# Two mixture-of-experts routers: what is gathered, in which precision, and in what portions

## The chip, the core and the metric

The kernel runs on one core of one Trainium2 chip. The metric is device time in microseconds (us) of one launch. The kernel before took 1326.77 us, the median of three runs (1324.72, 1326.77, 1327.38). Each traced run is one execution recorded by the hardware profiler.

## The reference

Two stacked transformer blocks work on 256 tokens of width 1024. Each block ends in a hierarchical mixture of experts (MoE). What matters here is that MoE; block 1 has 16 experts with hidden width 256, block 2 has 32 experts with hidden width 512:

```
h   = rms_norm(x) * gain (+ shift in block 2)
g   = softmax(h @ w_group + b_group)          # 4 groups, the best one is taken, p_g its probability
e   = h @ w_router + b_router                 # experts of that group only; the two best, softmax of the two
out = sum over the two experts:  p_g * p_e * (silu(h @ w_gate[e]) * (h @ w_up[e])) @ w_down[e]
x   = x + (gate of the block) * out
```

`rms_norm(x)` is x times r, where r = 1/sqrt(mean(x^2) + eps), one number per token. It is the "root" of this case. Block 2 takes the adaptive gains, shifts and gates of its norms from a conditioning vector, by twelve products with a 1024 x 6144 matrix that are here called ada jobs.

## The kernel before, in words

**Order of the work.** Block 1 mixes (0 to 137 us), adds `w_out` (to 148), routes (to 173) and runs its MoE (to 308). Block 2 mixes until 837 us, routes until 859 and runs its MoE until 1312; a final norm ends the program. Every engine runs its instructions in the order in which a scheduler put them; `with after(i):` pins an instruction behind another. SP (SyncE) issues the weight transfers one after the other in a fixed order (`Stream.ahead`, `Stream.take`). Each is a 1 MB tile that goes to one of 19 buffers of 8 KB a partition, tag `g8`; in the same 19 lie x, the transposed h (`hTm`), `xnl` and `XT`. A transfer waits until its buffer's last reader is done. A second pool, `st4`, has 4 smaller buffers.

**A router** (`Router`, then the head of `moe`). x is transposed on TensorE (`ptm`) and evicted as `hTm`; `plg` are the logits; DVE works out r (`rsqrt`) and applies it to the logits (`lg`). A chain of some 20 small DVE operations finds the two experts of a token (`f1m`, `f1o`, `f2m`, `f2o`) and ends in the one-hot rows `Mr` (L1013). TensorE counts places with `Mr`: `ppos`, five fp32 matmuls against a triangle and a matrix of ones. An fp32 matmul stands as two rows of TensorE in the trace, an fp32r matmul or a transpose as one; the text calls such a row a pass. From `ppos` comes `pe`, the place of a token in its expert's 64 slots or -1.

**Dispatch** (`places`, `dispatch`). `Dd` is a one-hot matrix (token by slot) from comparing `pe` with a row of numbers. `pgx` multiplies x*r by `Dd`, so each expert's tokens stand transposed in `XT`. x*r is carried as two fp32r halves, `xnh` (ACT, L956, after r) and the rest `xnl` (POOL, L1029 and L1030, for one half of the tokens, DVE, L1034, for the other). Four experts (a quad, two pairs) are dispatched at a time: 4 PSUM tiles x 2 x 4 matmuls of 256 columns, so 32 passes. `pgt` transposes `Dd` back into `Gt`, and `pws` gathers the weights of the slots (`ws`).

**Pairs.** For each pair of experts PE does gate (`pgg`, `pgu` in block 1), the turn of the previous pair's activations (`pactT`), its `pdn`, then up (`pgu`) and the combination of the previous pair (`py`, L1203). Behind each second pair stands the next dispatch. Two matrices of 256 x 4 KB of `XT` alternate.

**Ada jobs** (`ada_job`, L600). `pada` leaves four partial sums on four groups of partitions; ACT copies them (`adap`), four transposes `pac` (four more, `paq`, with columns taken in steps of four, in four of the jobs) turn them, and DVE reduces and adds. Six jobs run in block 1's mixing, three around the first router, three in block 2's mixing.

Of the kernel before, what the change touches and what calls it, by code (L numbers as in the profile page):

```python
# [10 lines left out]
F32 = mybir.dt.float32  # L11
# [10 lines left out]
D = 1024  # L22
KD = 8
# [45 lines left out]
C1_N = C_MB + 1024  # L69
# [3 lines left out]
def _consts():  # L73
# [11 lines left out]
    c[:, C_IOTA:C_IOTA + 64] = np.arange(64)  # L85
# [37 lines left out]
def _body(es, tc, I, cst_d, msk_d, out_d, tap, stop):  # L123
# [43 lines left out]
    ones = cst[:, C_ONE:C_ONE + 128]  # L167
# [281 lines left out]
    class Router:  # L449


        def __init__(self, x, E, gw, gb, ew, eb, gcol, bcol):
            self.x, self.E, self.gcol = x, E, gcol
            wr = self.wr = S("wr", [KD, 36], bufs=1)
# [5 lines left out]
            self.hTm = None  # L460
# [8 lines left out]
        def half(self, n):  # L469
# [131 lines left out]
    def ada_job(jobs, b, step=False):  # L601
# [4 lines left out]
        def run(t0, t1):  # L606
# [10 lines left out]
            q = mm_ps("pac", (4, 4, 32))  # L617
# [16 lines left out]

    fgq = by_four("fgq", I["ffn_norm_g"][0])
# [23 lines left out]
    for b in range(ADA1):  # L659
        ada_job(J1, b)  # L660
    for n in range(2):
        J1.row32(I["w_out"][0], 512 * n, lambda: mix[0],
               lambda j, p, n=n: V.tensor_tensor(x1[j][:, 512 * n:512 * n + 512], p,
                                                 xr[j][:, 512 * n:512 * n + 512], op=ALU.add))
# [8 lines left out]
    A.dma_start(cst[:, C_J:C_N], cst_d[:, C_J:C_N])  # L673
    J1.ahead(2)
# [41 lines left out]
    lam = S("lam", [1], bufs=1)  # L716

# [181 lines left out]
    def both(*gens):  # L899
        gens = list(gens)  # L900
        while gens:
            for g in list(gens):
# [22 lines left out]
    x1 += xt_  # L925
    st1.ahead(PRE1)
    drain(J1.run(2))
    rt = Router(x1, 16, I["router_g_w"][0], I["router_g_b"][0], I["router_e_w"][0], I["router_e_b"][0],
                colA[:, oFG:oFG + 8], None)
    for n in range(2):  # L930
        rt.half(n)
    for n in range(2):
        rt.logits(n)
# [5 lines left out]
    def moe(x, E, router, gcol, bcol, st, FE, n_static, mid=None, before_if=None, gain=None, idle=None):  # L939
# [5 lines left out]
        xh = [sp.tile([128, 2, 512], F32R, tag="st4", name="xnh", bufs=NST).rearrange("p a b -> p (a b)")  # L945
              for _ in range(2)]
        xl = R2("xnl", F32R)
        def q4(v, n=2):

            return v.rearrange("p (h k c) -> p h c k", h=n, k=4)  # L950

        def c4(v, n=2):
            return v.rearrange("p (h c k) -> p h c k", h=n, k=4)

        for i in (1, 0):
            A.activation(q4(xh[i]), c4(x[i]), AF.Copy, scale=r[:, i:i + 1])  # L956
# [37 lines left out]
        V.tensor_reduce(gpr, gx, op=ALU.add, axis=AX.X)  # L994
        V.reciprocal(gpr, gpr)
# [9 lines left out]
        w1 = S("w1", [2])  # L1005
        V.tensor_scalar(w1, e2, 1.0, None, op0=ALU.add)
        V.reciprocal(w1, w1)
        V.tensor_tensor(w1, w1, gpr, op=ALU.mult)
        V.tensor_tensor(e2, e2, w1, op=ALU.mult)
        pe = S("pe", [2, 40], bufs=1)  # L1010
        we = S("we", [2, 40], bufs=1)
        M = S("Mr", [2, E], bufs=1)
        last_m = V.tensor_tensor(M, oh1, oh2, op=ALU.add)  # L1013
        V.tensor_tensor(oh1, oh1, b3(w1, E), op=ALU.mult)
        V.tensor_tensor(oh2, oh2, b3(e2, E), op=ALU.mult)
        V.tensor_tensor(we[:, :, 0:E], oh1, oh2, op=ALU.add)

        ppx = mm_ps
        pp = ppx("ppos", (3, E))
        lt = cst[:, C_LT:C_LT + 128]  # L1020
        mm(pp[:, 0, :], lt, M[:, 0, :], True, True)
        mm(pp[:, 1, :], lt, M[:, 1, :], True, False)
        mm(pp[:, 1, :], ones, M[:, 0, :], False, True)
        mm(pp[:, 2, :], ones, M[:, 0, :], True, False)
        pos = mm(pp[:, 2, :], ones, M[:, 1, :], False, True)
        for n in range(2):
            cs = slice(512 * n, 512 * n + 512)
            t = W("xn", [512])
            G.tensor_scalar(t, x[1][:, cs], r[:, 1:2], None, op0=ALU.mult)  # L1029
            G.tensor_tensor(q4(xl[1][:, cs], 1), c4(t, 1), q4(xh[1][:, cs].bitcast(F32), 1), op=ALU.subtract)  # L1030
        with after(last_m):
            for n in range(2):
                cs = slice(512 * n, 512 * n + 512)
                V.scalar_tensor_tensor(q4(xl[0][:, cs], 1), c4(x[0][:, cs], 1), r[:, 0:1],  # L1034
                                       q4(xh[0][:, cs].bitcast(F32), 1), op0=ALU.mult, op1=ALU.subtract)
# [4 lines left out]
        V.scalar_tensor_tensor(pe[:, :, 0:E], pp[:, 0:2, :], 1.0, M, op0=ALU.add, op1=ALU.mult)  # L1040
        V.tensor_scalar(pe[:, :, 0:E], pe[:, :, 0:E], 1.0, None, op0=ALU.subtract)
# [4 lines left out]
        def spill():  # L1046
# [28 lines left out]
            V.tensor_scalar(s2_, s2_, -float(CAP), 1.0 - CAP, op0=ALU.mult, op1=ALU.add)  # L1075
# [6 lines left out]
            V.tensor_scalar(pe[:, :, E:NE], pe[:, :, E:NE], 1.0, None, op0=ALU.subtract)  # L1082
# [4 lines left out]
        def places(e0, n):  # L1087
            d = W("Dd", [2, n, 64], F32R)
            it = cst[:, C_IOTA:C_IOTA + 64].unsqueeze(1).to_broadcast([128, n, 64])
            for i in range(2):  # L1090
                V.tensor_tensor(d[:, i], it, pe[:, i, e0:e0 + n].unsqueeze(2).to_broadcast([128, n, 64]), op=ALU.is_equal)
            return d

        def dispatch(e0, n, xt=None, d=None, late=None):
# [935 lines left out]
```

## Time and profile before

| | us |
|---|---|
| median of 3 runs | 1326.77 |
| the profiled execution | 1325.01 |
| its span in the trace | 1323.2 |
| TensorE (PE) busy | 1249.6 (94%) |
| VectorE (DVE) busy | 661.7 (50%) |
| ScalarE (ACT) busy | 425.1 (32%) |
| GpSimd (POOL) busy | 38.7 (3%) |

The profiled execution took 1.8 us more than its span. Shares are averages over stages: DVE is half busy in all, but it is the only engine that works in parts of the routers, and TensorE's 94% covers the stages where it sets the pace as well as the last one, where the DMA engines are full.

### The profile page before, as it was taken

Reading aid. Unit: us, or ns where it says so; the run is one execution under the profiler, and the core shown is the slowest. Engines: PE = TensorE matmul, PEld = TensorE weight load, DVE = VectorE, ACT = ScalarE, POOL = GpSimd, SP = SyncE. Lnnn points to the kernel's source line nnn. Section 1 sums busy time; section 2 is a strip of 40 time slices with the busy share of each in tenths; the row PEclk is TensorE's granted clock in tenths of the full one; section 3 lists DMA queues with packets and bytes.
Section 4 is the critical chain, followed back from the end, with each engine's and each line's share of the span. In section 5 each row is a group of like instructions: output and inputs, shape, how many; then the busy total and the mean of one; then the engine's idle time right before and its main releaser. Section 6 shows DMA issues by size and latency. Waiting matters only on the chain. (4 is left out here: it accounts for less than half of the span.)

```text
span 1323.2 us, 19925 instructions
## 1 busy us (share of the span) xinstructions
PE 1249.6 (94%) x8098; PEld 852.3 (64%) x8098; DVE 661.7 (50%) x1442; ACT 425.1 (32%) x728; POOL 38.7 (3%) x50
## 2 busy tenths in 40 slices
PE   6988999999999999999999999899999998999886
PEld 5845566666788998898989889734435454444432
DVE  6895641115569987876575866632212222121213
ACT  5734312224234565544434443311111111011102
POOL 4110100000000000000000000100000000000000
PEclk9989999999999999999999999899999999999998
DMA  9798789993433231352525676799999999999994
GB/s 275 249 328 317 248 329 360 392 353 116 147 94 95 66 112 53 98 162 65 160 69 177 211 262 266 284 372 422 421 421 422 422 421 421 421 422 422 421 422 159
DMA packets 124355, 359.79 MB, mean 272 GB/s; under 512 B 15272, under 2 KB 64593, under 8 KB 97632
## 3 DMA queue, kind: packets, MB, share of 16 engines
q1 hardware_dynamic: 114224, 355.49, 70.7%
q10 hardware_dynamic: 9024, 2.24, 0.8%
q8 instruction: 67, 1.10, 0.3%
q0 software_dynamic: 1008, 0.70, 0.2%
q14 instruction: 32, 0.26, 0.1%
HBM read 357.35 MB, written 1.05 MB: 271 GB/s over the span
## 5 line engine op out<-in xcount | busy, mean ns | idle before, releaser
L156 PE MATMUL pg<-hT,hi 128*128 128x256 f32 (+1 forms) x1024 | 232.6, 321 | 1.5 <-DVE Qg L1373 1.5
L156 PE MATMUL pgu<-w,XT 128*64 128x256 f32 (+1 forms) x1088 | 186.4, 481 | 10.5 <-DMA w<-in_w_up_dram 10.5
L156 PEld LDWEIGHTS pg<-hT,hi 128*128 128x128 f32 x1024 | 167.2, 188 | 16.4 <-DVE Qg L1373 1.7
L236 DVE TENSOR_TENSOR lo<-w,hi 128x1024 fp32r<-128x1024 f32 x122 | 146.0, 1219 | 45.2 <-ACT hi L235 17.3
L156 PE MATMUL pdn<-w,actT 128*64 128x512 f32 x656 | 153.4, 597 | 14.9 <-ACT actT L1180 14.9
L156 PE MATMUL pg<-hT,lo 128*128 128x256 f32 (+1 forms) x512 | 162.4, 318 | 0.0
L235 ACT ACTIVATE hi<-w 128x1024 fp32r<-128x1024 f32 x122 | 125.3, 1053 | 93.4 <-PE pr L156 32.3
L156 PEld LDWEIGHTS pgu<-w,XT 128*64 128x64 f32 x1088 | 87.1, 137 | 103.2 <-issue 62.8
L156 PE MATMUL pgg<-w,XT 128*64 128x512 f32 x512 | 117.4, 596 | 1.0 <-DMA w<-in_w_gate_dram 1.0
L156 PEld LDWEIGHTS pdn<-w,actT 128*64 128x64 f32 x656 | 56.7, 136 | 94.6 <-issue 71.6
L156 PEld LDWEIGHTS pg<-hT,lo 128*128 128x128 f32 x512 | 96.3, 188 | 7.3 <-issue 0.4
L156 PE MATMUL pr<-hi,hT 128*128 128x256 f32 (+1 forms) x384 | 88.9, 321 | 0.6 <-PEq L1282 0.6
L156 PEld LDWEIGHTS pgg<-w,XT 128*64 128x64 f32 x512 | 37.1, 137 | 70.3 <-issue 63.9
L1169 DVE SCALAR_TENSOR_TENSOR act<-sgm,ws,pgu 128x512 f32<-128x512 f32 (+1 forms) x25 | 24.4, 975 | 103.1 <-PE pgu L156 103.1
L1195 DVE TENSOR_TENSOR Pg<-pdn,g 128x512 f32<-128x512 f32 x32 | 22.0, 689 | 98.4 <-PE pdn L156 98.4
L1161 DVE TENSOR_TENSOR sgm<-sgm,pgg 128x512 f32<-128x512 f32 x16 | 11.0, 688 | 117.1 <-ACT sgm L1160 117.0
L156 PEld LDWEIGHTS pr<-hi,hT 128*128 128x128 f32 x384 | 64.1, 188 | 7.2 <-issue 1.0
L1160 ACT ACTIVATE sgm<-pgg 128x512 f32<-128x512 f32 x16 | 9.6, 598 | 177.4 <-PE pgg L156 177.4
L1199 ACT ACTIVATE Ph<-Pg 128x512 fp32r<-128x512 f32 x32 | 20.1, 630 | 135.0 <-DVE Pg L1195 135.0
L156 PE MATMUL pr<-lo,hT 128*128 128x256 f32 (+1 forms) x192 | 61.8, 322 | 0.0
L156 PE MATMUL pgx<-Dd,xnh 128*128 128x256 f32 (+1 forms) x208 | 49.8, 284 | 0.1
L156 PE MATMUL pgx<-Dd,xnl 128*128 128x256 f32 (+1 forms) x208 | 49.6, 283 | 0.0
(520 smaller groups left out, 1927.5 us busy)
## 6 DMA issues: line engine op xcount, KB each, us to landing
w<-in_w_gate_dram SPq DMA_DIRECT2D x82, 1024.0 KB, 19.7
w<-in_w_up_dram SPq DMA_DIRECT2D x82, 1024.0 KB, 19.6
w<-in_w_down_dram SPq DMA_DIRECT2D x80, 1024.0 KB, 19.8
w<-in_w_in_dram SPq DMA_DIRECT2D x98, 512.0 KB, 4.6
w<-in_w_ada_dram SPq DMA_DIRECT2D x24, 1024.0 KB, 6.8
w<-in_w_out_dram SPq DMA_DIRECT2D x4, 1024.0 KB, 5.3
w<-in_w_branch_b_dram SPq DMA_DIRECT2D x8, 512.0 KB, 4.1
w<-in_w_branch_a_dram SPq DMA_DIRECT2D x8, 512.0 KB, 4.3
```

Source lines behind the costliest of these rows:

```text
L156: t2["mm"] = PE.matmul(out, lhsT, rhs, start=start, stop=stop, skip_group_check=True)
L235: t2["hi"] = A.activation(hi[:, ks], t, AF.Copy)
L236: t2["lo"] = V.tensor_tensor(lo[:, ks], t, hi[:, ks].bitcast(F32), op=ALU.subtract)
L1160: A.activation(sg, outs[0], AF.Sigmoid)
L1161: V.tensor_tensor(sg, sg, outs[0], op=ALU.mult)
L1169: V.scalar_tensor_tensor(act.rearrange("p (f c) -> p c f", f=NF), sg.rearrange("p (c f) -> p c f", f=NF), wcol, o.rearrange("p (c f) -> p ...
L1195: V.tensor_tensor(qg, q, gain[:, n, :], op=ALU.mult)
L1199: A.activation(ph, q, AF.Copy)
```

## The change

In the first router (`split=True`) x itself, without r, is split into `xnh` and `xnl`, on ACT and DVE, while the logits are made; the first half of x is transposed and split inside the second `w_out` job. r goes along as a third column of the gathered weights, and comes back as `rs`, one number per slot: the sigmoid's scale, a factor of its product, and a factor of `ws`. In the second router nothing is split: `pgx` multiplies fp32 x, read with columns in steps of four, by an fp32 `Dd` that holds r where it held 1, for one pair at a time. `XT` of the second moves to `st4`. The counting matmuls are fp32r, the row of numbers starts at 1 so `pe` is one operation, and the weights are worked out behind the first `Dd`. `pac` and `paq` become fp32 matmuls against a two-column matrix that sums as it turns.

```
@@ class Router @@
+            if split:
+                self.xh = [sp.tile([128, 2, 512], F32R, tag="st4", name="xnh", bufs=NST) ... for _ in range(2)]
+                self.xl = R2("xnl", F32R)
+                self.hTm = U("hTm", [KD, 256])
...
+            if self.xh:
+                for i in range(2):
+                    with after(ev):
+                        A.activation(self.part(self.xh[i], n), self.turned(i, n), AF.Copy)
+                    if n == 0:
+                        t1["rest"] = self.rest(i, n)
...
+        def rest(self, i, n):
+            return V.tensor_tensor(self.part(self.xl[i], n), self.turned(i, n),
+                                   self.part(self.xh[i].bitcast(F32), n), op=ALU.subtract)
@@ ada_job @@
-                PE.transpose(q[:, c].rearrange("p j a -> p (j a)"), pt[:, 128 * c:128 * c + 128], ident)
-            V.tensor_reduce(ada[:, 4 * b:4 * b + 4, :], q.rearrange("p c j a -> p c a j")[:, :, 0:2, :], op=ALU.add, axis=AX.X)
+                mm(q[:, c], pt[:, 128 * c:128 * c + 128], sel2, True, True)
@@ moe @@
-        for i in (1, 0):
-            A.activation(q4(xh[i]), c4(x[i]), AF.Copy, scale=r[:, i:i + 1])
...
-            G.tensor_scalar(t, x[1][:, cs], r[:, 1:2], None, op0=ALU.mult)
-            G.tensor_tensor(q4(xl[1][:, cs], 1), c4(t, 1), q4(xh[1][:, cs].bitcast(F32), 1), op=ALU.subtract)
...
-                V.scalar_tensor_tensor(q4(xl[0][:, cs], 1), c4(x[0][:, cs], 1), r[:, 0:1],
-                                       q4(xh[0][:, cs].bitcast(F32), 1), op0=ALU.mult, op1=ALU.subtract)
...
+        M = S("Mr", [2, E], F32R, bufs=1)
...
-        V.scalar_tensor_tensor(pe[:, :, 0:E], pp[:, 0:2, :], 1.0, M, op0=ALU.add, op1=ALU.mult)
-        V.tensor_scalar(pe[:, :, 0:E], pe[:, :, 0:E], 1.0, None, op0=ALU.subtract)
+        V.scalar_tensor_tensor(pe[:, :, 0:E], pp[:, 0:2, :], 1.0, M.bitcast(F32), op0=ALU.add, op1=ALU.mult)
...
+            if xl is None:
+                d = W("Dd", [2, n, 64])
+                for i in range(2):
+                    for q in range(n):
+                        t2["dd"] = V.tensor_scalar(d[:, i, q, :], it, pe[:, i, e0 + q:e0 + q + 1], r[:, i:i + 1],
+                                                   op0=ALU.is_equal, op1=ALU.mult)
...
+                xts[b] = (U("XT", [KD, 256]) if xl else
+                          sp.tile([128, KD, 128], F32, tag="st4", name="XT", bufs=NST))
...
+            if xl is None:
+                for h in range(2):
+                    p = mm_ps("pgx", (4, w))
+                    for k in range(4):
+                        for i in range(2):
+                            mm(p[:, k, :], x[i].rearrange("p (h c k) -> p h k c", h=2, k=4)[:, h, k, :],
+                               d[:, i].rearrange("p n c -> p (n c)"), i == 0, i == 1)
+                    for k in range(4):
+                        evict(xt[:, 4 * h + k, 0:w], 4 * h + k, p[:, k, :], k % 2)
...
-            A.activation(sg, outs[0], AF.Sigmoid)
-            V.tensor_tensor(sg, sg, outs[0], op=ALU.mult)
+                A.activation(sg, outs[0], AF.Sigmoid, scale=rs)
+                V.scalar_tensor_tensor(sg, outs[0], rs, sg, op0=ALU.mult, op1=ALU.mult)
...
-        quads = list(range(0, E + n_static, 4))
+        step = 4 if xl else 2
+        quads = list(range(0, E + n_static, step))
```

How the instructions move is shown at three places. In the second MoE, TensorE's order over one period of two pairs; before, from an up to the second gate behind it (the 32 `pgx` matmuls in turn are left out after the first two):

```order
L156 MATMUL pgu<-w,XT 64x512 x16
L156 MATMUL py<-Ph,Gt 128x512 x2
L156 MATMUL py<-Pl,Gt 128x512 x2
L156 MATMUL py<-Ph,Gt 128x512 x2
L156 MATMUL py<-Pl,Gt 128x512 x2
L156 MATMUL pgg<-w,XT 64x512 x16
L1177 MATMUL pactT<-cst,act 128x128 x4
L156 MATMUL pdn<-w,actT 64x512 x16
L156 MATMUL pgu<-w,XT 64x512 x16
L156 MATMUL py<-Ph,Gt 128x512 x2
...
L156 MATMUL pgx<-Dd,xnh 128x256
L156 MATMUL pgx<-Dd,xnl 128x256
```

and now, the same engine and place:

```order
L156 MATMUL pgu<-w,XT 64x512 x16
L156 MATMUL py<-Ph,Gt 128x512 x2
L156 MATMUL py<-Pl,Gt 128x512 x2
L156 MATMUL py<-Ph,Gt 128x512 x2
L156 MATMUL py<-Pl,Gt 128x512 x2
L156 MATMUL pgx<-Dd,x_1222 128x128 x16
L1206 MATMUL pgt<-cst,Dd 128x128 x2
L156 MATMUL pws<-we,Dd 128x2 x2
L156 MATMUL pgg<-w,XT 64x512 x16
L1260 MATMUL pactT<-cst,act 128x128 x4
L156 MATMUL pdn<-w,actT 64x512 x16
```

A dispatch of 16 fp32 matmuls (32 passes) with its `pgt` and `pws` stands ahead of every gate but the first, where one of 32 fp32r matmuls stood ahead of each second.

In the second router, DVE's order from the end of the expert search to the first one-hot rows; before:

```order
L1013 TENSOR_TENSOR Mr<-f1o,f2o 128x64
L1034 SCALAR_TENSOR_TENSOR xnl<-x_1224,rry,xnh 128x128x4
L994 TENSOR_REDUCE gpr<-gx 128x2
L1006 TENSOR_SCALAR w_8490<-e_8487 128x2
L1034 SCALAR_TENSOR_TENSOR xnl<-x_1224,rry,xnh 128x128x4
L995 RECIPROCAL gpr<-gpr 128x2
L1007 RECIPROCAL w_8490<-w_8490 128x2
L1040 SCALAR_TENSOR_TENSOR pe<-ppos,Mr 128x2x32
```

and now:

```order
L1033 TENSOR_TENSOR Mr<-f1o,f2o 128x64
L1050 SCALAR_TENSOR_TENSOR pe<-ppos,Mr 128x2x32
L1130 TENSOR_SCALAR Dd<-cst,pe,rry 128x64 x4
L1054 TENSOR_REDUCE gpr<-gx 128x2
L1060 TENSOR_TENSOR sm<-ms,rry 128x2
```

The two `xnl` and the weights no longer stand between `Mr` and the first `Dd`.

In the first router, TensorE's order between the logits and the dispatch; before:

```order
L156 MATMUL plg<-wr,hTm 128x20 x16
L156 MATMUL pada<-w,scp 32x512 x8
L619 MATMUL pac<-cst,adap 128x128 x4
L627 MATMUL paq<-cst,adap 128x128 x4
L156 MATMUL pada<-w,scp 32x512 x8
L619 MATMUL pac<-cst,adap 128x128 x4
L627 MATMUL paq<-cst,adap 128x128 x4
L156 MATMUL pada<-w,scp 32x512 x4
L156 MATMUL ppos<-Mr,cst 128x16 x5
L156 MATMUL pada<-w,scp 32x512 x4
L156 MATMUL pgx<-Dd,xnh 128x256
```

and now:

```order
L156 MATMUL plg<-wr,hTm 128x20 x8
L492 MATMUL ptm<-cst,x_1222 128x128 x8
L156 MATMUL plg<-wr,hTm 128x20 x8
L156 MATMUL pada<-w,scp 32x512 x8
L156 MATMUL pac<-cst,adap 128x2 x4
L156 MATMUL paq<-cst,adap 128x2 x4
L156 MATMUL pada<-w,scp 32x512 x8
L156 MATMUL pac<-cst,adap 128x2 x4
L156 MATMUL paq<-cst,adap 128x2 x4
L156 MATMUL pada<-w,scp 32x512 x4
L156 MATMUL ppos<-Mr,lto 128x16 x5
L156 MATMUL pgx<-Dd,xnh 128x256
```

Two and a half ada jobs stand ahead of `ppos` as before; the other half job now comes inside the first dispatch, and half of the transposes `ptm` has moved ahead of the logits, into `w_out`.

## Rows read from the trace of the kernel before

**Rows 1.** Windows: stretch; busy us (instructions) of PE, PEld, DVE, ACT, POOL; PEclk; DMA share; GB/s.
```profile
850.00:860.00 10.00, 10.00 (x50) 7.83 (x51) 8.18 (x32) 2.82 (x5) 0.00 (x0) 0.68 0.41 147
860.00:870.00 10.00, 10.00 (x54) 4.00 (x52) 6.58 (x19) 1.33 (x2) 0.00 (x0) 1.00 0.64 253
870.00:1000.00 130.00, 126.51 (x626) 54.30 (x624) 30.06 (x48) 16.49 (x28) 0.00 (x0) 1.00 1.01 421
```

**Rows 2.** Timeline of SP's queue: start, us of the group, issues; second MoE.
```profile
854.02 12.17 SPq L224 DMA_DIRECT2D w<-in_w_up_dram  x4
...
1186.00 7.76 SPq L224 DMA_DIRECT2D w<-in_w_gate_dram  x4
...
1215.91 7.78 SPq L224 DMA_DIRECT2D w<-in_w_gate_dram  x4
```

**Rows 3.** Timeline of PE: start, busy us, passes [idle before]; second MoE's last two pairs.
```profile
1268.71 7.53 PE L156 MATMUL pgg<-w,XT 128*64 128x512 f32 x31
...
1299.70 7.14 PE L156 MATMUL pdn<-w,actT 128*64 128x512 f32 x32
...
1311.27 1.05 PE L156 MATMUL py<-Pl,Gt 128*128 128x512 f32 x2
```

**Rows 4.** Timeline of PE: second router and first pair.
```profile
849.68 2.34 PE L156 MATMUL ppos<-Mr,cst 128*128 128x32 f32 x10 [3.31 <-DVE Mr L1013]
...
858.76 7.09 PE L156 MATMUL pgg<-w,XT 128*64 128x512 f32 x32
...
867.01 7.09 PE L156 MATMUL pgu<-w,XT 128*64 128x512 f32 x32
```

**Rows 5.** Timeline of DVE and POOL: second router, the search of the experts.
```profile
843.54 0.69 DVE L997 TENSOR_TENSOR lg<-lg,fgo 128x64 f32<-128x64 f32 x1
...
845.29 1.31 DVE L984 TENSOR_TENSOR f1o<-f1o,f1c 128x64 f32<-128x64 f32 x1
846.63 1.45 DVE L1000 SCALAR_TENSOR_TENSOR lg<-f1o,lg 128x64 f32<-128x64 f32 x1
...
849.14 0.23 DVE L984 TENSOR_TENSOR f2o<-f2o,f2c 128x64 f32<-128x64 f32 x1
...
845.00 3.00 POOL L1030 TENSOR_TENSOR xnl<-xn,xnh 128x512 fp32r<-128x512 f32 x2
```

**Rows 6.** Timeline of PE: two pairs of the second MoE, the second with a dispatch.
```profile
903.12 7.09 PE L156 MATMUL pgg<-w,XT 128*64 128x512 f32 x32
...
927.41 7.09 PE L156 MATMUL pgg<-w,XT 128*64 128x512 f32 x32
...
949.65 0.73 PE L156 MATMUL py<-Ph,Gt 128*128 128x512 f32 x2
...
951.60 0.28 PE L156 MATMUL pgx<-Dd,xnh 128*128 128x256 f32 x1
...
955.38 0.27 PE L1131 MATMUL pgt<-cst,Dd 128*128 128x128 f32 x1
...
956.55 3.65 PE L156 MATMUL pgg<-w,XT 128*64 128x512 f32 x16
```

**Rows 7.** Timeline of PE: passes of 128 columns, contiguous and stepped, and narrow ones.
```profile
325.22 3.73 PE L156 MATMUL ptr<-rdg,x 128*128 128x128 f32 x32
...
732.47 0.64 PE L627 MATMUL paq<-cst,adap 128*128 128x128 f32 x4
...
839.95 1.98 PE L156 MATMUL plg<-wr,hTm 128*128 128x36 f32 x16 [0.24 <-ACT hTm L488]
```

**Rows 8.** By tile: weight loads of `pac` and `paq`: ns min/median/max, starts.
```profile
L619 PEld LDWEIGHTS pac<-cst,adap x48: 137/141/231, 76.8 to 786.4; 128*128 128x128 f32 x48
...
L627 PEld LDWEIGHTS paq<-cst,adap x16: 196/210/226, 158.6 to 732.7; 128*128 128x128 f32 x16
```

**Rows 9.** Timeline of PE: first router and the first gate of its MoE.
```profile
166.95 1.29 PE L156 MATMUL ppos<-Mr,cst 128*128 128x16 f32 x10
...
173.22 3.67 PE L156 MATMUL pgu<-w,XT 128*64 128x256 f32 x32
```

More of the change, by code (lines that the diff above doesn't have):

```diff
@@ L925, in _body @@
     x1 += xt_
-    st1.ahead(PRE1)
[L927 to L933, printed above, removed]
+    rt = Router(x1, 16, I["router_g_w"][0], I["router_g_b"][0], I["router_e_w"][0], I["router_e_b"][0],
+                colA[:, oFG:oFG + 8], None, True)
+    st1.ahead(PRE1 - 2)
+    drain(J1.run(1))
+    job = J1.run(1)
+    next(job)
+    next(job)
+    with after(t2["mm"]):
+        rt.half(0)
+    with after(rt.tr):
+        next(job)
+    st1.ahead(PRE1)
+    drain(job)
+    rt.logits(0)
+    rt.half(1)
+    rt.logits(1)
     tap("x1", x1[0])
@@ L944, in moe @@
         plg = router.last
[L945 to L953, printed above, removed]
-        for i in (1, 0):
-            A.activation(q4(xh[i]), c4(x[i]), AF.Copy, scale=r[:, i:i + 1])
+        xh, xl = router.xh, router.xl
         for i in range(2):
@@ new lines, in dispatch @@
+            if xl is None:
+                for h in range(2):
[6 more added lines that the diff above has]
+                        evict(xt[:, 4 * h + k, 0:w], 4 * h + k, p[:, k, :], k % 2)
+            else:
+                for kk in range(4):
+                    p = mm_ps("pgx", (2, w))
+                    for j in range(2):
+                        k = 2 * kk + j
+                        for q, (s, i) in enumerate(((xh, 0), (xl, 0), (xh, 1), (xl, 1))):
+                            mm(p[:, j, :], s[i][:, 128 * k:128 * k + 128], d[:, i].rearrange("p n c -> p (n c)"),
+                               q == 0, q == 3)
+                    for j in range(2):
+                        evict(xt[:, 2 * kk + j, 0:w], 2 * kk + j, p[:, j, :], late is not None and j)
@@ L1216, in ex @@
                                   skip_runtime_bounds_check_because="a sum over one-hot rows of expert numbers below E")
-        quads = list(range(0, E + n_static, 4))
+        step = 4 if xl else 2
+        quads = list(range(0, E + n_static, step))
         late = []
-        nxt = dispatch(0, 4, late=late)
-        ei = spill()
+        d = places(0, step)
+        if xl:
+            with after(t2["dd"]):
+                router.rest(1, 1)
+        weights(t2["dd"])
+        nxt = dispatch(0, step, d=d, late=late)
+        with after(t2["dd"]):
+            ei = spill()
         act = None
@@ L1243, in moe @@
                     st.add_pair(ex(2 * p), ex(2 * p + 1))
-                sg, o = gate(st.take(p, "g"), xt, 128 * a)
+                sg, o = gate(st.take(p, "g"), xt, 128 * a, rs[:, a:a + 1] if rs is not None else None)
                 parts = None
@@ L1298, in nest @@
                             q += 1
-                sg, o = gate(out["g"], xt, 0)
+                sg, o = gate(out["g"], xt, 0, rs[:, 0:1] if rs is not None else None)
                 act = up(out["u"], xt, 0, sg, o, ws[:, 0:1])
```

217 lines of the change are left out of this document (127 added, 90 removed).

## The prediction, made before the change ran

> **What bounds the kernel now.** I read first the windows over the second MoE, because it is a third of the program. From 870 us on the DMA engines' share is 1.01, while just before it is 0.41 and 0.64 [rows 1]: here transfers set the pace, and they had idled 5.9 + 3.6 = 9.5 us in the twenty us before. SP's queue says how fast the pace is and why it idled: gate tiles of one pair and of the next are issued 1215.91 - 1186.00 = 29.9 us apart, 2.49 us for each of twelve tiles; but the four up tiles at 854.02 took 12.17 us to issue [rows 2], the first behind x's buffer, which `py` still read, the others behind the first gate. TensorE's timeline gives its own need before transfers hold it: 24.29 us from gate to gate without a dispatch, 29.14 with one, the mean 26.7 [rows 6]. So each pair PE gains 3.2 us on the transfers, eats up the lead, and waits at the end. The last gate starts at 1268.71 and the last combination ends at 1312.3 [rows 3]. Elsewhere PE sets the pace: after the first router no transfer is waited for until block 2, and in both routers DVE's chain of small operations does, with PE idle 3.31 us ahead of the second `ppos` [rows 4].
>
> The span is 1323.2 us, the profiled execution 1325.01, the median of the runs 1326.77. I sum against 1325.01 and add the 1.8 us between it and the median at the end. Less than 0.2%, 2.65 us, is what a measurement of this kernel can't tell from no change.
>
> **Second router: earlier.** POOL's `xn` and `xnl` go. While they ran, three operations on 128x64 took 0.69, 1.31 and 1.45 us where a like one took 0.23 [rows 5]: 2.8 us. `ppos` can then start at 849.68 - 2.8 = 846.9, and PE's idle time is 0.5 us instead of 3.31. Behind that idle time the granted clock was 0.68 in the mean of 850 to 860, a mix of 1.2 and 2.4 GHz [rows 1, 4]; with a sixth of the gap I take the full level to be held. `ppos` falls from ten passes in 2.34 us [rows 4] to five at 0.118 and a drain, 0.8; `pe` and the first two `Dd` 0.7, with the two `xnl` no longer queued ahead of them on DVE; 32 `pgx` passes 3.8 (955.38 - 951.60 [rows 6], the same count). That is the first gate at 852.2 instead of 858.76, 6.5 us earlier. If the clock falls as before, `ppos` takes half of its 2.34, and the 6.7 us from its end to the gate stay: 854.8, 4 us earlier. On the other side 7.
>
> **Second MoE: what a dispatch costs.** Each pair now has 16 fp32 matmuls, 32 passes of 128 columns, and half of the 1.17 us of `pgt` and `pws` [rows 6]. 32 fp32 passes of 128 columns with a contiguous weight took 3.73 [rows 7], 0.117 each, as much as a pass of 256 columns in the old dispatch, 0.118 [rows 6]: halving the columns gives nothing back, so a pair pays what a quad paid. The weights are now read in steps of four columns; the only rows that do so are the transposes `paq`. Their loads are recorded longer, 210 against 141 ns [rows 8], but four passes took 0.64 [rows 7]; less 0.28 for the last pass, three steps of 0.12. I take 3.7 us for the passes (3.57 at 0.1116, the step of the contiguous row without its last pass's tail, to 3.85 at 0.12), with 0.59 a dispatch of 4.3, and a pair of 24.29 + 4.3 = 28.6 (28.4 to 28.75).
> The Trainium skill ("TensorE: Matmul & The Clock Gate", LDWEIGHTS) says that a weight load takes the stationary's columns divided by 1.2, in ns, here 107, whatever is streamed. The contiguous row stands 10% above that, and by the page alone the passes of a pair would be an estimated 3.4 us and the end some 4 us earlier. The rule counts columns and not their step, so it speaks against the slow rival below, and against any gain from 128 columns in place of 256.
>
> Does something else wait? DVE's up product and four `Dd` are to be ready before `pgx`. The combination before it covers 951.60 - 949.65 = 1.95 us [rows 6], in which the product and the two larger `Dd` were ready before; I count no wait, up to 0.3. The first pair has no combination: up to 2.0 bare, and I count it. `XT` is evicted by ACT and DVE in turn; the gate needs one eighth each 0.86 us (7.09 / 8), and has 0.59 us of `pgt` and `pws` ahead: no wait.
>
> So: first gate 852.2; to up 867.01 - 858.76 = 8.25 [rows 4] less 0.59; up 7.0; bare wait 2.0; dispatch 4.3: second gate at 873.2. Fourteen pairs of 28.6: the last gate at 1273.6. Behind it PE needs a pair, 24.3, the last down and its combination, 1312.3 - 1299.7 = 12.6 [rows 3], and about 1 for the turn, 38 in all; before it took 43.6 with waits for transfers. End at 1311.6, against 1312.3: **-0.7 us**. Do transfers allow it? Two more buffers are there for weights (`XT` leaves two, `xnl` and the late x balance), 5 us of transfers, and the first gate frees the next 6.5 us earlier; of the 9.5 idle us 5 to 9.5 go, and transfers alone would end the stage at 1303 to 1307. PE's pair of 28.6 lies under their 29.9, but it starts so far behind that it is late last: the bound changes from DMA to PE. Range of the term: 15 dispatches of +-0.15 us, the gate 4 to 7 us earlier: -4 to +4.
>
> **First router.** The wide ACT and POOL work on x*r after r goes, and the split lies beside the logits. But PE's order keeps two and a half ada jobs ahead of `ppos`. Their `pac` and `paq` grow from four passes to eight narrow ones: 1.98 / 16 = 0.124 each [rows 7], 0.99 against 0.48, four times +0.5, which eats most of what ACT, no longer busy, gives the job's copy. I put `ppos` at 165.4 instead of 166.95 [rows 9]; then 0.8, 1.1 for `pe` and `Dd`, 3.75 for 32 passes, and 0.95 for the half ada job that now stands inside them: first gate 172.0 against 173.22. Behind it `pgt` alone takes 0.6 less, but `pws` has moved ahead, some 0.4 of it beside `Dd`. I take **-1.4 us**, from 0 (DVE waits in order on the jobs' sums between its searches) to -3.5 (the search ends 2 us earlier as in the second router and `ppos` follows it). The MoE's quads are the same work.
>
> **Ada jobs elsewhere.** Three in block 2's mixing, where PE is the engine that is waited for, have three `pac` and one `paq`: 4 x 0.5 less 0.2 for DVE's shorter sum: **+1.8**. Six in block 1 lie where PE waits for others: 0 to 3, **+0.5**.
>
> **Sum.** -0.7 - 1.4 + 1.8 + 0.5 = +0.2 on 1325.0; with the 1.8 to the median 1327; the bare wait of 2.0 is taken at its upper end, so I take 1 off and say **1326 us, no change**, 1322 to 1331 for this case alone.
>
> **Rivals.**
> *PE keeps up and the transfers' gain is real* (faster). For it: the passes may go at 0.1116 (-2), the gate may come 7 us earlier (-0.5), the first router may give its 3.5 (-2), the early ada jobs nothing (-0.5), and the bare wait half (-1): 1320. Against: each is its end of a range. It ends where transfers do, some 6 us below the forecast.
> *Stepped weights set the pass* (slower). In `pgx` the load of 128 stepped columns isn't hidden: at the recorded 0.210 a pass a dispatch costs 32 x (0.210 - 0.116) = 3.0 us more, in 15 of them 45: 1371. Each ns of a pass is 0.48 us of the end, so from 0.122 on the kernel is measurably slower. For it: 210 against 141 ns [rows 8]. Against: the step of `paq`, 0.12, in one group of four.
> *Waits around each single dispatch* (slower). There are twice as many handovers: DVE's `Dd` behind the up product, `XT` through two engines, PSUM buffers. At 0.5 us a pair 7.5 us: 1333. Against: the covers counted above. It decides from 0.2 us a pair.
> *Nothing in the first router*: `ppos` stays where it was; +1.4, inside the forecast's range.
>
> **Chances.** The forecast 0.55, of which 0.19 lies below -2.65 us, 0.24 within, 0.12 above; PE keeps up 0.23; stepped weights 0.11; waits 0.11. Faster 0.42, within 0.24, slower 0.34. Range 1318 to 1337: it takes in the fast rival, the waits, and a stepped pass up to 0.14, and leaves out the wholly unhidden load.
>
> **What would show it.** In the profile after: the second router's 128x64 operations at 0.23; PE's gap before `ppos` under 1 us and a clock of 1.00 behind it; the first gate near 852; `pgx` 32 passes in 3.7; gates 28.6 apart with no waits for transfers, the last near 1273.6; the first MoE's gate near 172. The prediction is wrong if PE still waits for weights at the end (then the fast rival), if gates stand over 28.9 apart, or if the mixing of block 2 moves by more than 2.5 us.

## The result, and the profile after

The changed kernel takes 1408.29 us (median of four runs, 1407.37 to 1409.09) against 1325.74 for the kernel before on the same chip: a ratio of 1.0622, 95% interval 1.0601 to 1.0643. It is 82.5 us slower. The forecast was 1326, its range 1318 to 1337, and the slow rival it names (1371) is also short of it. Two of the signs by which the prediction called itself wrong are there: gates stand 32.2 us apart (over 28.9), and block 2's mixing moved by 5.0 us (over 2.5).

Where the time went is read from starts of the same instructions on TensorE in the two traces (spans 1323.2 and 1405.6 us):

| mark on PE | before | after | later by | lost in the stage |
|---|---|---|---|---|
| `ptr<-rdg,xc`, end of block 1's mixing | 130.30 | 133.59 | 3.3 | 3.3 |
| first gate of the first MoE | 173.22 | 188.34 | 15.1 | 11.8 |
| `ptr<-rdg,x`, start of block 2 | 325.22 | 344.21 | 19.0 | 3.9 |
| last logits of the second router | 839.95 | 863.96 | 24.0 | 5.0 |
| first gate of the second MoE | 858.76 | 880.11 | 21.4 | -2.7 |
| end of the span | 1323.2 | 1405.6 | 82.4 | 61.0 |

The second MoE first. The timeline of PE in the profile after, columns as in [rows 6], shows the first two gates, one period, and the last gate:

```profile
863.96 1.98 PE L156 MATMUL plg<-wr,hTm 128*128 128x36 f32 x16 [0.24 <-ACT hTm L496]
...
870.83 0.73 PE L156 MATMUL ppos<-Mr,lto 128*128 128x32 f32 x5 [0.46 <-DVE Mr L1033]
...
872.45 7.73 PE L156 MATMUL pgx<-Dd,x 128*128 128x128 f32 x32
880.11 7.09 PE L156 MATMUL pgg<-w,XT 128*64 128x512 f32 x32
...
904.79 7.09 PE L156 MATMUL pgg<-w,XT 128*64 128x512 f32 x32
...
929.00 7.50 PE L156 MATMUL pgx<-Dd,x 128*128 128x128 f32 x32
936.33 0.38 PE L1206 MATMUL pgt<-cst,Dd 128*128 128x128 f32 x2
936.55 0.51 PE L156 MATMUL pws<-we,Dd 128*128 128x2 f32 x4
936.99 7.09 PE L156 MATMUL pgg<-w,XT 128*64 128x512 f32 x32
...
1356.09 7.09 PE L156 MATMUL pgg<-w,XT 128*64 128x512 f32 x32
```

The 32 passes of a dispatch take 936.33 - 929.00 = 7.33 us, 0.229 each, where the 32 of a quad took 3.78 [rows 6] and the forecast had 3.7. Gates stand 936.99 - 904.79 = 32.20 apart, and in the mean of fourteen pairs (1356.09 - 904.79) / 14 = 32.24. In the groups of the profile's page no gate or up waits for weights any more (before, gates waited 1.0 us for them and ups 10.5). The bound did change from transfers to PE, as forecast, but PE's pair is 32.2, not 28.6. The loads behind those passes, by tile over the same dispatch (ns, min/median/max), answer to [rows 8]:

```profile
L156 PEld LDWEIGHTS pgx<-Dd,x x32: 308/330/330, 928.8 to 936.0; 128*128 128x128 f32 x32
L156 PE MATMUL pgx<-Dd,x x32: 272/397/397, 929.0 to 936.1; 128*128 128x128 f32 x32
```

A load takes 330 ns in the record; the contiguous ones took 188 to 192. The second router's search on DVE, in answer to [rows 5], is what was forecast: 0.23 us for each of the three operations that had taken 0.69, 1.31 and 1.45.

```profile
867.46 0.23 DVE L1024 TENSOR_TENSOR lg<-lg,fgo 128x64 f32<-128x64 f32 x1
...
868.74 0.23 DVE L1013 TENSOR_TENSOR f1o<-f1o,f1c 128x64 f32<-128x64 f32 x1
869.00 0.23 DVE L1027 SCALAR_TENSOR_TENSOR lg<-f1o,lg 128x64 f32<-128x64 f32 x1
...
871.86 0.98 DVE L1130 TENSOR_SCALAR Dd<-cst,pe,rry 128x64 f32<-128x64 f32 x4
```

From the last logits to the first gate it is now 880.11 - 863.96 = 16.15 us, of which `pgx` is 7.7; before it was 18.81. The first router, PE's timeline after, in answer to [rows 9]:

```profile
165.87 1.05 PE L156 MATMUL pac<-cst,adap 128*128 128x2 f32 x8 [0.72 <-ACT adap L643]
166.79 2.00 PE L156 MATMUL paq<-cst,adap 128*128 128x2 f32 x8
168.72 3.53 PE L156 MATMUL pada<-w,scp 128*32 128x512 f32 x16
172.98 1.05 PE L156 MATMUL pac<-cst,adap 128*128 128x2 f32 x8 [0.73 <-ACT adap L643]
173.89 2.00 PE L156 MATMUL paq<-cst,adap 128*128 128x2 f32 x8
175.83 1.94 PE L156 MATMUL pada<-w,scp 128*32 128x512 f32 x8
177.69 1.24 PE L156 MATMUL ppos<-Mr,lto 128*128 128x16 f32 x5
...
188.34 3.67 PE L156 MATMUL pgu<-w,XT 128*64 128x256 f32 x32
```

Two things are to be seen. `paq`, eight narrow passes that read `adap` in steps of four, takes 2.00 us, 0.25 a pass, where `pac` beside it, contiguous, takes 1.05. And the same `pada` matmuls need 3.53 us for sixteen passes where 1.92 sufficed before: the clock. The windows of after (columns as in [rows 1]) say which level was granted:

```profile
160.00:170.00 10.00, 9.28 (x48) 5.30 (x51) 3.58 (x21) 1.74 (x4) 0.00 (x0) 0.67 0.90 267
170.00:180.00 10.00, 8.44 (x42) 4.64 (x35) 3.39 (x14) 0.80 (x2) 0.00 (x0) 0.67 0.90 339
180.00:190.00 10.00, 10.00 (x64) 7.59 (x66) 6.38 (x33) 3.19 (x5) 0.00 (x0) 0.72 0.52 195
190.00:200.00 10.00, 9.50 (x62) 6.76 (x60) 4.38 (x16) 0.96 (x2) 0.00 (x0) 0.83 0.55 210
```

The kernel before was at 0.83 from 150 to 170 and at 1.00 from there. A window of 10 us mixes two levels, 1.2 GHz (0.50) and 2.4 GHz (1.00). Shorter ones of after, between the rows of `paq` (at 166.79, 173.89, 194.10 and, in block 2, 751.74):

```profile
166.00:168.00 2.00, 2.00 (x14) 2.00 (x14) 0.17 (x1) 0.00 (x0) 0.00 (x0) 1.00 1.22 231
169.00:171.00 2.00, 2.00 (x12) 0.40 (x8) 1.73 (x11) 0.20 (x1) 0.00 (x0) 0.50 1.09 364
172.00:175.00 3.00, 2.27 (x17) 2.02 (x13) 0.27 (x2) 0.60 (x1) 0.00 (x0) 1.00 1.05 405
176.00:185.00 9.00, 8.17 (x35) 4.55 (x32) 4.91 (x27) 0.47 (x1) 0.00 (x0) 0.50 0.53 211
186.00:195.00 9.00, 8.50 (x70) 6.82 (x68) 6.86 (x25) 3.39 (x6) 0.00 (x0) 1.00 0.49 178
196.00:199.00 3.00, 3.00 (x15) 1.76 (x17) 0.16 (x1) 0.00 (x0) 0.00 (x0) 0.50 0.87 363
...
753.00:759.00 6.00, 6.00 (x57) 5.71 (x57) 4.83 (x8) 0.97 (x2) 0.00 (x0) 0.50 0.27 79
```

So the clock isn't low throughout: it has come back to 1.00 each time, and falls to 0.50 anew right behind each of the four rows of `paq`.

### The profile page after: what moved, and what is told of

The parts are those of the page before. It is cut to its first block, busy times and chain, and to the rows that moved or that the text cites. A ratio compares the mean times of both kernels' runs of the same rounds, so it can differ in the third digit from the quotient of the medians.

```text
span 1405.6 us, 20679 instructions
## 1 busy us (share of the span) xinstructions
PE 1342.5 (96%) x8408; PEld 950.1 (68%) x8408; DVE 676.4 (48%) x1536; ACT 432.6 (31%) x761; POOL 26.3 (2%) x42
## 3 DMA queue, kind: packets, MB, share of 16 engines
HBM read 357.35 MB, written 1.05 MB: 255 GB/s over the span
## 5 line engine op out<-in xcount | busy, mean ns | idle before, releaser
L156 PE MATMUL pgu<-w,XT 128*64 128x256 f32 (+1 forms) x1088 | 180.3, 484 | 0.2 <-PE pgt L1206 0.2
L156 PEld LDWEIGHTS pg<-hT,hi 128*128 128x128 f32 x1024 | 169.1, 190 | 16.2 <-DVE Qg L1463 1.7
L156 PE MATMUL pdn<-w,actT 128*64 128x512 f32 x656 | 146.9, 597 | 15.1 <-ACT actT L1263 15.1
L156 PEld LDWEIGHTS pgx<-Dd,x 128*128 128x128 f32 x512 | 120.6, 329 | 3.9 <-issue 2.5
L156 PE MATMUL pgx<-Dd,x 128*128 128x128 f32 x512 | 120.5, 395 | 1.7 <-DVE Dd L1130 1.7
L156 PEld LDWEIGHTS pdn<-w,actT 128*64 128x64 f32 x656 | 51.5, 136 | 94.6 <-issue 73.8
L156 PE MATMUL pgg<-w,XT 128*64 128x512 f32 x512 | 113.4, 595 | 0.0
L1149 ACT ACTIVATE XT<-pgx,adaq,mod2q 128x128 f32<-128x128 f32 x64 | 29.3, 458 | 216.4 <-PE pgx L156 200.2
L1145 DVE TENSOR_SCALAR XT<-pgx,mod2q,adaq 128x128 f32<-128x128 f32 x64 | 26.1, 408 | 80.0 <-ACT XT L1149 80.0
## 6 DMA issues: line engine op xcount, KB each, us to landing
w<-in_w_gate_dram SPq DMA_DIRECT2D x82, 1024.0 KB, 10.5
```

The source lines that it names most:

```text
L156: t2["mm"] = PE.matmul(out, lhsT, rhs, start=start, stop=stop, skip_group_check=True)
L1145: V.tensor_scalar(xt, p, gcol[:, k:k + 1], bcol[:, k:k + 1], op0=ALU.mult, op1=ALU.add)
L1149: A.activation(xt, p, AF.Identity, scale=gcol[:, k:k + 1], bias=bcol[:, k:k + 1])
```

## The experiments

All comparisons are with the kernel before, run on the same chip; its median was 1323 to 1325 us there. "Ratio" is to that kernel, with its 95% interval; e1, e7 and e8 ran once, and are read by their passes and stages. The question for the second MoE was whether the step of the columns makes the pass dear, or fp32 at 128 columns; for the rest, whether the ada jobs or the split cost.

**e1_forms: four steps in one run.**

```
-    mm(p[:, k, :], x[i].rearrange("p (h c k) -> p h k c", h=2, k=4)[:, h, k, :],
+    mm(p[:, k, :], col(x[i], 4 * h + k, (4, 2, 1, 8)[e0 // 8 % 4]),     # col: 128 columns of x in steps of s
```

> The changed kernel, but the second MoE's dispatch reads the stationary columns of x in steps of 4, 2, 1 and 8 by turns (pairs 0-3, 4-7, 8-11, 12-15); with other steps than 4 other columns of x are gathered, so the output is another. Theory A (a stepped fp32 weight load sets the pass): the 32 passes of a dispatch take 7.3 us at step 4 and 8 and about 3.7 at step 1, with step 2 between or at 7.3; gates 32.2 apart at step 4, 28.6 at step 1; in all 14 us under the changed kernel's 1408, or 29 if step 2 is cheap as well. Theory B (an fp32 pass of 128 columns costs 0.23 in this loop, whatever the step): 7.3 us in all four, 1408.

1382.95 us in one run, 25 us under the changed kernel (29 were expected if step 2 is cheap; block 1's mixing ended 3.4 us later in it). One dispatch at each of the steps 4, 2, 1 and 8, in PE's timeline of this run:

```profile
932.64 7.50 PE L156 MATMUL pgx<-Dd,x 128*128 128x128 f32 x32
...
1025.77 3.94 PE L156 MATMUL pgx<-Dd,x 128*128 128x128 f32 x32
...
1140.33 3.77 PE L156 MATMUL pgx<-Dd,x 128*128 128x128 f32 x32
...
1258.29 7.66 PE L156 MATMUL pgx<-Dd,x 128*128 128x128 f32 x32
```

Theory A. One column in four and one in eight cost twice what one in one and one in two do; steps of 8 bytes are nearly free (3.94 against 3.77 us), steps of 16 and 32 bytes are not. All columns here are of four bytes, so bytes and elements can't be told apart.

**e4_perm: the same result, contiguous.** ACT writes a copy `xp` of x in the dispatch's order while the logits are made, in the place where the first router's split stands.

```
+            if self.xp:
+                for i in range(2):
+                    with after(ev):
+                        A.activation(self.part(self.xp[i], n), self.turned(i, n), AF.Copy)
-    mm(p[:, k, :], x[i].rearrange("p (h c k) -> p h k c", h=2, k=4)[:, h, k, :],
+    mm(p[:, k, :], router.xp[i][:, 512 * h + 128 * k:512 * h + 128 * k + 128],
```

> The changed kernel with an fp32 copy of x in the order of the dispatch's columns, written by ACT while the second router's logits are made, so that the dispatch reads contiguous weights; the same result. Theory A (the step alone): dispatch 3.7 us instead of 7.3, gates 28.6 apart, 16 x 3.6 = 58 us less: 1351, with no waits for weights. Theory B (fp32 at 128 columns is what costs): no gain, 1408; copies of 4 x 0.7 us on ACT may even delay the router by 1 to 2 us.

1350.67 us, ratio 1.0192 (1.0149 to 1.0235): 57.6 us come back by the medians, and 58 were expected; its two runs lie 5.8 us apart (1347.78 and 1353.56), so the closeness is in part luck. PE's timeline of the faster one:

```profile
863.94 1.98 PE L156 MATMUL plg<-wr,hTm 128*128 128x36 f32 x16 [0.24 <-ACT hTm L497]
...
872.43 3.84 PE L156 MATMUL pgx<-Dd,xp 128*128 128x128 f32 x32
876.20 7.09 PE L156 MATMUL pgg<-w,XT 128*64 128x512 f32 x32
...
896.99 7.09 PE L156 MATMUL pgg<-w,XT 128*64 128x512 f32 x32
...
925.47 7.09 PE L156 MATMUL pgg<-w,XT 128*64 128x512 f32 x32
```

From the logits to the gate 876.20 - 863.94 = 12.26 us, the first pair 20.8, the next 28.5: the forecast had 12.25 (839.95 to 852.2), 21.0 and 28.6.

**e2_ada: the ada jobs as before**, the diff of `pac` and `paq` undone.

```
-                mm(q[:, c], p4[:, c, :], sel2, True, True)
+                PE.transpose(q[:, c].rearrange("p j a -> p (j a)"), p4[:, c, :], ident)
```

> The changed kernel with the ada jobs as before (transposes, then a DVE reduce and add). Theory A (the jobs' fp32 matmuls are on the path everywhere, pac 0.4 and paq, stepped, 1.4 dearer each): 12 x 0.4 + 4 x 1.4 = 10 us less, a little under that where PE waits: 1399; the first router's ppos 4 us earlier after the same w_out end. Theory B (the first router's loss comes from the split and its order; jobs hide elsewhere): at most 3 us less, 1405.

1387.96 us, ratio 1.0476 (1.0447 to 1.0505): 20.3 us come back, twice what I gave theory A. `ppos` starts at 169.95 and the first gate at 177.45. Read from starts, `pac` took 0.42 us more and `paq` 1.36 more than the transposes, so the jobs' own passes are 12 x 0.42 + 4 x 1.36 = 10.5 us, half of it; most of the other half goes with the clock behind them, as the next run shows. Block 2's mixing takes 514.5 us here, as before (514.7), so all of the 5.0 us lost there is the jobs'.

**e10_paq: only the stepped `paq` as before**, `pac` left as an fp32 matmul.

> The changed kernel with only the stepped ada products paq taken back to transposes and a DVE reduce; the contiguous pac stay fp32 matmuls. Theory A (the stepped narrow passes cost most, by their own 1.4 us each and by the low clock behind them): 12 to 16 of the 20 us that all the ada jobs gave back, 1392 to 1396, and the clock back to 1.00 by 185 us. Theory B (narrow fp32 passes cost, stepped or not): 8 us or less, over 1400.

1393.88 us, ratio 1.0524 (1.0501 to 1.0547): 14.4 of the 20.3 us are `paq`'s. Theory A; windows of this run, against those of after above:

```profile
160.00:170.00 10.00, 8.57 (x57) 3.85 (x57) 5.22 (x28) 1.49 (x4) 0.00 (x0) 0.81 0.91 258
170.00:180.00 10.00, 9.16 (x77) 6.79 (x77) 7.35 (x38) 2.73 (x5) 0.00 (x0) 1.00 1.04 411
180.00:190.00 10.00, 9.50 (x84) 6.55 (x82) 5.68 (x20) 1.42 (x3) 0.00 (x0) 1.00 0.77 294
190.00:200.00 10.00, 9.43 (x72) 4.83 (x68) 1.87 (x3) 1.94 (x4) 0.00 (x0) 1.00 0.99 389
```

In 1 us windows of this run the clock is at 1.00 from 164 us on, and it is 1.00 in 740 to 760: behind none of the four rows of transposes does it fall, though `pac`, narrow fp32 too but contiguous, stands ahead of each. Four `paq` are 4 x 1.36 = 5.4 us of passes; the other 9 us go with the lower clock, which in the changed kernel falls behind each of the first three, the last time until 199 us, and once more, at 0.83 in 740 to 760, behind the fourth. An estimate from the windows agrees: from 160 to 200 us the clock falls short of the full level by 11.1 us in the changed kernel (the sum of 10 x (1 - PEclk)) and by 1.9 here, a difference of 9.2 us if PE is always busy. What it is in these passes that the clock falls behind isn't shown. Their own 2.00 us are not the clock's: in e3 the first `paq` ran at 0.50 and took 1.99.

**e3_order: the split kept, but out of the `w_out` job**, and the second half's addition not pinned.

```
-    next(job)
-    with after(t2["mm"]):
-        rt.half(0)
...
+    drain(J1.run(2))
+    for n in range(2):
+        rt.half(n)
```

> The changed kernel with the first router's split kept, but nothing of it placed inside the second w_out job and the second half's x addition not pinned behind the split's rest. Theory A (the placement costs: x's second half waits 1.2 us for DVE, the logits end later, and the clock stays low longer): 2 to 4 us less, 1404 to 1406. Theory B (the placement is neutral; ada jobs in front of ppos set the gate): within 1 us of 1408.

1408.09 us, ratio 1.0634 (1.0595 to 1.0672). The median is the changed kernel's, but the four runs span 1405.36 to 1412.99, so the time alone can't tell theory A's 2 to 4 us from nothing. The trace speaks for theory B: its first gate is at 187.07, 1.3 us earlier, but the mixing in front of it also ended 0.7 earlier, which leaves 0.6 us.

**e5_perm_ada: e2 and e4 together.**

> The changed kernel with both mended: an fp32 copy of x in the dispatch's order, so that weights are contiguous, and the ada jobs as before. Theory A (the step in the dispatch and the jobs' matmuls are separate costs that add): 1408 - 57.5 - 20.3 = 1330. Theory B (they overlap, since the end of the second MoE is bound by transfers in part): 1335 or more. Either way the rest over the kernel before, some 7 us, is then the first router's, its gate at 177 instead of 173, and the pairs' 28.5 us on PE.

1328.61 us (seven runs), ratio 1.0025 (1.0012 to 1.0038). The two causes add: 79.7 of the 82.5 us, where the two runs apart gave 57.6 + 20.3 = 77.9. What is left over the kernel before is 3.9 us by the medians (1324.71 on this chip), 3.3 by the ratio.

**e7_paq32: a long row of stepped transposes** in the kernel before, to see why four of them had misled me.

```
-                for c in range(4):
-                    PE.transpose(q[:, c].rearrange("p j a -> p (j a)"), p4[:, c, :], ident)
+                for c in range(32):
+                    PE.transpose(q[:, c % 4].rearrange("p j a -> p (j a)"), p4[:, c % 4, :], ident)
```

> The kernel before, with each paq done with 32 transposes instead of 4 (each of the four eight times over, same result), to see a long row of stepped weight loads in transposes. Theory A (the four passes that the prediction rested on were too few: loads ran ahead, a long row goes at 0.23): 32 passes in 7.3 us. Theory B (a transpose, one pass for an fp32 element, loads stepped columns at the full pace, and the two-pass matmul is different): 3.8 us.

1337.43 us in one run. One of the four rows, and its loads by tile:

```profile
742.02 4.00 PE L627 MATMUL paq<-cst,adap 128*128 128x128 f32 x32
```

```profile
L627 PEld LDWEIGHTS paq<-cst,adap x32: 197/209/212, 741.9 to 745.6; 128*128 128x128 f32 x32
```

Theory B: (4.00 - 0.28) / 31 = 0.120 us a pass. Four passes were not too few. A transpose takes its stepped operand at the pace of contiguous columns, and a matmul on the same tile, with the same step (`paq` of after, 0.25), does not. The load is recorded longer at this step here too (209 ns against 140 for `pac` beside it), so the stepped tile is what is loaded; the passes are not held up by it.

**e8_f32r_step: stepped columns in one-pass fp32r** matmuls of 256 columns, in the kernel before, `xnh` and `xnl` being written in x's own order.

```
-                        mm(p[:, j, :], s[i][:, 128 * k:128 * k + 128], d[:, i]...
+                        mm(p[:, j, :], c4(s[i])[:, k // 4, k % 4, :], d[:, i]...      # c4: columns in steps of four
```

> The kernel before, but with xnh and xnl written in the order of x, and the dispatch reading them in steps of four columns, as fp32r in one pass of 256 columns each; the same result. Theory A (a step of 16 bytes sets the load's pace whatever the matmul's kind): 32 passes in 7.3 us instead of 3.75, 13 quads: the first MoE 16 us longer, the second hidden in part behind transfers, 1340 to 1355. Theory B (only the two-pass fp32 matmul is hurt): 3.75 us, within 2 us of the kernel before.

1349.04 us in one run. First and last pass of a quad's 32, and what follows:

```profile
236.31 0.39 PE L156 MATMUL pgx<-Dd,xnl 128*128 128x256 f32 x1
...
243.31 0.39 PE L156 MATMUL pgx<-Dd,xnl 128*128 128x256 f32 x1
243.54 0.27 PE L1131 MATMUL pgt<-cst,Dd 128*128 128x128 f32 x1
```

Theory A: (243.31 - 236.31) / 30 = 0.233 us a pass in fp32r too, with twice the columns streamed, so the load sets the pace and not the stream. Block 2 starts 20.5 us later (345.7 against 325.2), and the whole is 24 us longer: of the 8 x 3.6 us more that the second MoE's dispatches take, nearly all lies in time in which PE had waited for transfers.

**e6_f32quads: one idea of the change alone.** x*r gathered in fp32, contiguous, four experts at a time, in the kernel before; POOL and DVE have no rest to make.

```
-                    for q, (s, i) in enumerate(((xh, 0), (xl, 0), (xh, 1), (xl, 1))):
-                        mm(p[:, j, :], s[i][:, 128 * k:128 * k + 128], d[:, i].rearrange("p n c -> p (n c)"),
-                           q == 0, q == 3)
+                    for i in range(2):
+                        mm(p[:, j, :], xh[i][:, 128 * k:128 * k + 128], d[:, i].rearrange("p n c -> p (n c)"),
+                           i == 0, i == 1)
```

> The kernel before, with one thing of the change taken over: x*r is gathered in fp32, not split, in both MoEs; ACT writes it as before in the dispatch's order, contiguous, and experts are dispatched four at a time as before (16 fp32 matmuls of 256 columns, 32 passes). The POOL and DVE operations for the rest go. Theory A (the router's gain is real and the loss is the step and the single pairs): a quad costs 3.75 us as before, the second gate comes 4 to 6 us earlier (near 853.5), transfers idle less, 1314 to 1322. Theory B (the earlier gate is given back, since transfers set the end): 1323 to 1326, no change.

1338.7 us, ratio 1.0108 (1.0091 to 1.0125): 1.1% slower, against both theories. The dispatch of a quad, in PE's timeline:

```profile
913.01 7.07 PE L156 MATMUL pgx<-Dd,xnh 128*128 128x256 f32 x32
919.91 0.38 PE L1120 MATMUL pgt<-cst,Dd 128*128 128x128 f32 x2
```

6.90 us, 0.216 a pass. With contiguous loads an fp32 pass of 256 columns takes 1.8 times as long as an fp32r pass of 256 (0.118), so it is not the load that sets it. The prediction's "halving the columns gives nothing back" compared an fp32 row with an fp32r row; within fp32 halving them takes the pass from 0.216 to 0.117. So fp32 gains little by quads: 3.45 us a pair, against 3.63 alone (e4, 924.82 - 921.19). The router's gain is there (17.3 us from the logits to the gate, 18.8 before); the loss lies ahead of it, block 2 starting 16.2 us later (2.7 of them from a later end of the mixing).

**e9_rest_dve: what the trace of before points at, alone.** fp32r quads, contiguous columns and ada jobs stay; POOL does nothing; the rest is made on DVE, in the second router one piece ahead of the places and three behind the first `Dd`, and the weights behind that.

```
-            G.tensor_scalar(t, x[1][:, cs], r[:, 1:2], None, op0=ALU.mult)
-            G.tensor_tensor(q4(xl[1][:, cs], 1), c4(t, 1), q4(xh[1][:, cs].bitcast(F32), 1), op=ALU.subtract)
+            for m in range(1 if E == 32 else 4):
+                rest(m % 2, m // 2)
...
+        d = places(0, 4)
+        with after(t2["dd"]):
+            for m in range(1 if E == 32 else 4, 4):
+                rest(m % 2, m // 2)
```

> The kernel before, with only what the second router's trace points at: no operation on POOL, the rest xnl on DVE alone (in the second router one piece ahead of the places and three behind the first Dd, in the first all four ahead of the places), the weights behind Dd. fp32r quads, contiguous columns and the ada jobs stay. Theory A (POOL beside DVE costs the search 2.8 us and the clock behind it more; the gate comes 3 to 5 us earlier and transfers, which then idle less, end the kernel earlier): gate 2 near 854.5, 1317 to 1322. Theory B (three pieces of 1.1 us behind Dd hold the dispatch up by what the search gains): gate within 1 us of 858.8, 1323 to 1326.

1319.51 us (six runs), ratio 0.9960 (0.9946 to 0.9974): 4.6 us faster than the kernel before, and so faster than both. Of this run, PE's timeline and the windows:

```profile
847.08 1.30 PE L156 MATMUL ppos<-Mr,cst 128*128 128x32 f32 x10 [0.50 <-DVE Mr L1006]
...
854.59 7.09 PE L156 MATMUL pgg<-w,XT 128*64 128x512 f32 x32
```

```profile
850.00:860.00 10.00, 9.31 (x56) 5.29 (x56) 9.47 (x31) 3.54 (x5) 0.00 (x0) 1.00 0.51 175
860.00:870.00 10.00, 10.00 (x54) 4.00 (x52) 5.37 (x15) 0.60 (x1) 0.00 (x0) 1.00 1.00 415
```

PE idles 0.50 us ahead of `ppos` instead of 3.31, the clock stays at 1.00, the gate comes 4.2 us earlier, and the transfers' idle time in these twenty us is 4.9 instead of 9.5 us [rows 1]: 4.6 us less, about what the kernel gains. Of the earlier gate, 2.8 us are won ahead of `ppos` (6.92 us behind the last logits, 9.73 before) and 1.6 behind it (7.51 to the gate, 9.08 before), where the clock and the new order of the weights can't be told apart. From 1000 us on it still waits 11.2 us for weights (11.5 before), so transfers set it.

## Why the prediction was wrong, point by point

**The step that failed: "less 0.28 for the last pass, three steps of 0.12. I take 3.7 us for the passes".** The row was read rightly and is no accident of four (e7). It was the wrong analog: `paq` before was a transpose, `pgx` after is a matmul, and only the transpose takes stepped columns at the pace of contiguous ones. The measured passes are 7.33 us a dispatch. Sixteen dispatches at 3.7 us more (7.33 against 3.63 in e4) are 59 us; e4 gave back 57.6 by the medians and 59.6 by the traced runs (1407.37 against 1347.78). The rival that had this mechanism was priced from the recorded load, 0.210; the load in a matmul is recorded at 330 ns, and the pass takes 0.229, so the rival's 45 us would have been 54. Its chance of 0.11 was too small: [rows 8] had shown that something happens at that step, and the only row against it was of another kind of instruction.

The page of the Trainium skill weighed there ("TensorE: Matmul & The Clock Gate", LDWEIGHTS) counts a load's columns and not their step. e1 settles that for this kernel: at equal columns, step 1 and 2 take 3.77 / 32 = 0.118 and 0.123 us a pass, step 4 and 8 take 0.234 and 0.239. Where the page and the measurement differ, the measurement decides. The contiguous passes, at 117 to 118 ns, stand 10% above the 107 ns that this page of the Trainium skill gives.

**The ada jobs.** I priced all new passes at 0.124 from `plg`. For `pac` that holds (1.05 us for eight). For `paq`, whose operand is stepped as `pgx`'s is, it was the same error a second time: 2.00 us instead of 0.99. And a second error lay in the sum: I counted the passes' own time alone, and put nothing for the clock. Behind each row of `paq` the granted clock falls to 0.50, and `pada`, `ppos`, the first half of the first dispatch and a part of the first up run at that level. The term was +2.3 elsewhere and +2.0 ahead of `ppos`; together they measured 20.3 (e2), of which `paq` 14.4 (e10).

**The first router.** Forecast 1.4 us earlier, it is 11.8 later within its stage. In e2, without the jobs' part, its gate is at 177.45, still 4.2 later than before, part of it from a later end of the mixing (132.9 against 130.3). Counted from the end of the mixing, its `ppos` is 0.4 us later than before (37.01 against 36.65), where 1.5 earlier was forecast, and from `ppos` to the gate it takes 7.50 us (6.27 before, 6.6 forecast). A single trace tells this stage to some 3 us only: e5, with the same block 1 as e2, has 39.73 to `ppos`. The placement inside `w_out` is not it (e3). That block 1's mixing ends later, by 3.3 us in the profile after, I can't put down to one edit: the traced runs of e1, e3 and e4, whose mixing is that of the changed kernel, ended it between 132.9 and 137.0, those of e6 to e9, whose mixing is that of before, between 129.9 and 133.0.

**What held.** The search of the second router lost its 2.8 us of delay, PE's gap is 0.46 us, the clock behind it 1.00, and from the logits to the gate it is 12.26 us with contiguous columns (e4), forecast 12.25. A pair with contiguous columns is 28.5, forecast 28.6. The first pair's bare wait, counted at 2.0, was 1.67. Evictions by two engines and single handovers cost nothing: the third rival did not appear. With both errors mended, e5 takes 1328.61 us where the sum stood at 1327 before I took 1 off, but that nearness is luck: 4.3 us of the sum (2.0 + 1.8 + 0.5) were for the jobs' new passes, which e5 does not have, so its other terms stood at 1323. In e5's trace the last logits of the second router start 6.9 us later than before (846.82), where those terms had them some 3 earlier; the router gives 6.6 back, as forecast, and from its gate to the end the second MoE takes 4.9 us more (469.3 against 464.4), where 5.8 was forecast. So the model of the second router and the second MoE was right but for one price; that of the first router was not. The bound did pass from transfers to PE; that is also why the earlier gate doesn't pay in this form, and does in e9, where each quad has one dispatch and not two.

**Open.** Why a transpose is spared; why the clock falls behind the stepped narrow passes; and which edit makes the 6.9 us that e5 loses ahead of the second router's last logits (e2, with the same block 1, loses 4.6 there).

## What to carry to other kernels

A price is taken from a row of the same kind of instruction, not only of the same engine, shape and step: a PE transpose is not a price for a matmul. Before a matmul reads its stationary operand in steps, ask how wide the step is: for columns of four bytes a step of two was nearly free here, and a step of four doubled the pass. A copy of 2 x 128x1024 by an idle ScalarE bought back some 58 us. And when an engine off the path shares its time with the one on it (POOL beside VectorE's small operations), taking its work away can shorten the path though it never stood on it.

## What the runs showed of the hardware that I had not expected

- Stationary columns of four bytes in steps of 1, 2, 4 and 8: 0.118, 0.123, 0.234, 0.239 us a pass of 128 columns (e1); 0.233 in fp32r with 256 columns streamed (e8); 0.120 in transposes at step 4 (e7).
- An fp32 pass of 256 columns takes 0.216 us, an fp32r one 0.118, both with contiguous loads (e6, [rows 6]).
- Behind each of four rows of eight narrow passes with stepped loads, 2 us each, the granted clock fell from 1.00 to 0.50; with transposes in their place it did not (e10).
- Three DVE operations on 128x64 took 0.69, 1.31 and 1.45 us while POOL worked on 128x512, and 0.22 to 0.23 us each in the two kernels in which POOL has no such work (after and e9).
